# Squares of the residual: two instructions of 2048 columns behind the first pair of column tiles, in place of eight of 512 inside it

## The chip, the cores and the metric

The kernel runs on one core of one Trainium2 chip. The metric is device time in microseconds (us) of one execution, as a median over several. A core has TensorE (PE, matmuls), VectorE (DVE), ScalarE (ACT), GpSimd (POOL) and SyncE (SP, which issues most DMAs). Each takes its own instructions strictly in the order in which the program was laid down; an instruction that waits holds up all that stand behind it on its engine.

## The reference

One decoder layer on 256 positions of 2048 channels in float32. The part that matters here is its second half:

```python
h = h + rms_norm(m @ w_out[l], post_mix_gain[l], NORM_EPS)
u = rms_norm(h, pre_ff_gain[l], NORM_EPS)
f = jnp.square(jax.nn.relu(u @ w_ff1[l])) @ w_ff2[l]
h = h + rms_norm(f, post_ff_gain[l], NORM_EPS)
```

`rms_norm(x, gain)` is x times gain divided by the root of the mean of the squares of x over the 2048 channels. For the second line the mean of h squared is wanted, one number for each of the 256 positions. `w_ff1` is 2048 x 8192, `w_ff2` 8192 x 2048.

## The kernel before, in words

Every float32 weight is used as a sum of two parts: ACT rounds it to a first part (`wh`, L141) and DVE takes the remainder (`wl`, L147), and TensorE multiplies with both. Weights come as chunks of 128 x 2048 (1 MB) from DRAM into one of three raw buffers; there are three buffers for `wh` and three for `wl`. In the first feed-forward product a chunk is a column tile: 128 of the 8192 output columns, over all 2048 channels. For each, PE does sixteen matmuls of 512 columns with `wh` (L272, the "high" half) and sixteen of 256 with `wl` (L276, the "low" half). Two column tiles make a pair (`ws_pair`, L267 to L281) that fills one PSUM tile `ps`; ACT and DVE then read it (L284, L285), and DVE multiplies it with `r2b`, the reciprocal root of the mean square (L877).

The norm's factor isn't applied to h ahead of the product, but to the product: so PE can start on the raw h. The first pair of column tiles, here called c0 and c1, is done in `stream` (L326 to L351), which for each of 16 blocks of 128 channels transposes h on PE (L333), scales it with the gain on ACT (L245) and DVE (L246), and multiplies (L260, L263). At fixed points in it `second_hook` (L688) puts other work: the last pieces of h itself on DVE (L681, `mix_out`), the split of the third column tile c2, and the squares: after every fourth block two ACT instructions over 512 columns each (`square`, L684), one for each half of the positions, whose sums land in `hss`. After the stream DVE adds up `hss` (L718), ACT takes the root (L315), DVE the reciprocal (L316) and a diagonal matrix from it (L722, `dg`); two small matmuls (L723) spread it over all partitions, and ACT copies it to `r2b` (L724).

The PSUM tile that L723 writes belongs to a pool that is closed right after (L729); its banks are then given to a new pool (L730), and from then on pairs take their PSUM tile from the old pool and the new one in turn. So a pair in the new pool can't start before L724 has read the factor; the pair behind it uses the old pool, and can start when the stream's own PSUM tile has been read (L284, L285).

Counting column tiles from c0: the stream does c0 and c1, the first pair behind it c2 and c3, the next ones c4 and c5, then c6 and c7, and so on.

Instructions marked with `pin` keep their order among themselves as written. All others are placed by a scheduler that simulates the program with estimated times when it is built, and lets an engine take a later piece of work first if by the estimate an earlier one would wait. The buffers for `wh` and `wl` are handed out in the order that it finds.

## Time and profile before

| what | us |
|---|---|
| median of 3 runs (1537.08 to 1538.44) | 1537.52 |
| the profiled execution, as timed | 1537.91 |
| its span, first to last instruction | 1536.1 |
| PE busy in it | 1519.5 |
| DVE busy | 1274.4 |
| ACT busy | 786.6 |

The busy time of an engine sums the durations of its instructions. A matmul's end is modelled, so neighbours overlap: a stretch in which PE is wholly busy can still differ in speed, which the granted clock and the distance between starts show. In a timeline each row is a run of like instructions: its start, how long it lasted, and in brackets how long the engine had idled before it and what ended that.

### The profile page before, as it was taken

The page shows a single profiled execution, that of the slowest core. Times are in us where ns is not written, and L with a number is a line of the kernel's source. Part 1 is how long each engine was busy: PE and PEld are TensorE (multiplying, and loading weights), DVE is VectorE, ACT ScalarE, POOL GpSimd, SP SyncE. Part 2 cuts the span into 40 slices and gives each one's busy share as a digit, 9 for nine tenths or more (in the row PEclk, how much of TensorE's full clock was granted, in tenths as well). Part 3 has the DMA queues.
Part 4 walks back from the last instruction along what each step waited for, and adds up shares of the span by engine and source line. Part 5 has one row for each costly group of instructions (what it writes and reads, how often), then busy time and mean ns, then how long its engine had stood idle before and what let it go on. Part 6 is the DMA issues. An engine that isn't in the chain of part 4 may idle for free.

```text
span 1536.1 us, 19418 instructions
## 1 busy us (share of the span) xinstructions
PE 1519.5 (99%) x7714; PEld 1293.0 (84%) x7714; DVE 1274.4 (83%) x1611; ACT 786.6 (51%) x857; POOL 42.2 (3%) x73
## 2 busy tenths in 40 slices
PE   9999999999999999999999999999999999999997
PEld 8888888888888888888887888888888888788885
DVE  8999999999999997956546888867887778867888
ACT  7544454655554545733435545644455445644454
POOL 0000000000000000000000000000011000110010
PEclk9999999999999999999999999999999999999999
DMA  8655555454544555575454654685478755795673
GB/s 325 221 192 187 185 186 184 167 189 165 192 165 169 205 202 192 186 280 184 180 194 168 247 179 184 215 271 189 166 223 269 225 185 185 238 294 192 233 228 129
DMA packets 51771, 313.66 MB, mean 204 GB/s; under 512 B 5728, under 2 KB 5856, under 8 KB 17248
## 3 DMA queue, kind: packets, MB, share of 16 engines
q1 hardware_dynamic: 44640, 290.40, 52.4%
q0 software_dynamic: 7040, 22.02, 6.1%
q8 instruction: 60, 0.98, 0.3%
q14 instruction: 31, 0.25, 0.0%
HBM read 295.62 MB, written 4.19 MB: 195 GB/s over the span
## 4 chain that ended last, share of the span: by engine, by line
PE 92%; DVE 3%; ACT 2%; issue 1%; DMA 0%; SPq 0%; DVEq 0%; ACTq 0%
PE ps L272 30%; PE ps L276 15%; PE ps L294 9%; PE ps L295 9%; PE ps L293 9%; PE ps L812 4%; PE ps L813 4%; PE ps L811 3%; DVE wl L147 2%; ACT wh L141 2%; PE ps L782 2%; PE ps L781 2%; PE ps L784 2%; PE po L548 1%; PE ps L260 1%
## 5 line engine op out<-in xcount | busy, mean ns | idle before, releaser
L141 ACT CAST wh<-raw 128x2048 fp32r<-128x2048 f32 (+1 forms) x256 | 456.6, 1790 | 487.5 <-PE ps L295 162.6
L147 DVE TENSOR_TENSOR wl<-raw,wh 128x2048 fp32r<-128x2048 f32 (+1 forms) x256 | 546.7, 2140 | 187.5 <-ACT wh L141 182.7
L272 PE MATMUL ps<-act,wh 128*128 128x512 f32 x1984 | 479.4, 392 | 0.0
L272 PEld LDWEIGHTS ps<-act,wh 128*128 128x128 f32 x1984 | 364.7, 188 | 70.1
L276 PEld LDWEIGHTS ps<-act,wl 128*128 128x128 f32 x1984 | 256.5, 191 | 10.0
L276 PE MATMUL ps<-act,wl 128*128 128x256 f32 x1984 | 263.8, 284 | 0.0
L294 PE MATMUL ps<-wl,act 128*128 128x512 f32 x624 | 243.8, 391 | 0.0
L293 PE MATMUL ps<-wh,act 128*128 128x512 f32 x624 | 243.7, 390 | 0.0
L295 PE MATMUL ps<-wh,act 128*128 128x512 f32 x624 | 243.6, 390 | 0.0
L462 DVE SCALAR_TENSOR_TENSOR y_all<-c,vec,y_all 128x256 f32<-128x256 f32 x480 | 210.1, 479 | 0.0
L294 PEld LDWEIGHTS ps<-wl,act 128*128 128x128 f32 x624 | 117.2, 188 | 24.1
L293 PEld LDWEIGHTS ps<-wh,act 128*128 128x128 f32 x624 | 117.2, 188 | 24.1
L295 PEld LDWEIGHTS ps<-wh,act 128*128 128x128 f32 x624 | 117.2, 188 | 24.0
L157 ACT CAST wh<-raw 128x1024 fp32r<-128x1024 f32 x64 | 65.3, 1051 | 91.2 <-PE ps L813 23.3
L812 PE MATMUL ps<-wl,g 128*128 128x512 f32 x256 | 101.4, 396 | 2.5 <-DVE wl L147 1.5
L813 PE MATMUL ps<-wh,g 128*128 128x512 f32 x256 | 99.8, 390 | 0.0
L811 PE MATMUL ps<-wh,g 128*128 128x512 f32 x256 | 99.7, 389 | 0.0
L782 PE MATMUL ps<-wl,gs 128*128 128x512 f32 x224 | 87.5, 391 | 0.6 <-DVE wl L158 0.5
L781 PE MATMUL ps<-wh,gs 128*128 128x512 f32 x224 | 87.2, 389 | 0.0
L784 PE MATMUL ps<-wh,gs 128*128 128x512 f32 x224 | 87.2, 389 | 0.0
L158 DVE TENSOR_TENSOR wl<-raw,wh 128x1024 fp32r<-128x1024 f32 x64 | 76.4, 1220 | 3.1 <-ACT wh L157 1.9
L157 ACT CAST wh<-sum 128x1024 fp32r<-128x1024 f32 x48 | 49.1, 1052 | 38.6 <-PE ps L272 14.3
(206 smaller groups left out, 1260.6 us busy)
## 6 DMA issues: line engine op xcount, KB each, us to landing
raw<-in_w_f_dram SPq DMA_DIRECT2D x124, 1024.0 KB, 5.0
raw<-in_w_q_dram SPq DMA_DIRECT2D x16, 1024.0 KB, 4.8
raw<-in_w_k_dram SPq DMA_DIRECT2D x16, 1024.0 KB, 4.8
raw<-in_w_v_dram SPq DMA_DIRECT2D x16, 1024.0 KB, 4.8
raw<-in_w_ga_dram SPq DMA_DIRECT2D x16, 1024.0 KB, 4.9
raw<-in_w_gc_dram SPq DMA_DIRECT2D x16, 1024.0 KB, 4.8
raw<-in_w_co_dram SPq DMA_DIRECT2D x16, 1024.0 KB, 4.8
raw<-in_w_o_dram SPq DMA_DIRECT2D x16, 1024.0 KB, 4.8
```

Of the source, the lines that this page charges most:

```text
L141: i = nc.scalar.copy(wh[:, a:b], raw[:, a:b])
L147: i = (eng or nc.vector).tensor_sub(wl[:, a:b], raw[:, a:b], wh[:, a:b].bitcast(F32))
L272: a = nc.tensor.matmul(ps[:, j], wh[:, k * P:(k + 1) * P], acts.both(k), start=(k == 0), stop=False)
L276: a = nc.tensor.matmul(ps[:, j, S:], wl[:, k * P:(k + 1) * P], acts.hi(k), start=False, stop=(k == KT - 1))
L293: nc.tensor.matmul(ps, acts.hi(k, a, b), wh[:, sl], start=(k == 0), stop=False)
L294: nc.tensor.matmul(ps, acts.hi(k, a, b), wl[:, sl], start=False, stop=False)
L295: nc.tensor.matmul(ps, acts.lo(k, a, b), wh[:, sl], start=False, stop=(k == KT - 1))
L462: i = nc.vector.scalar_tensor_tensor(y, c[:, j:j + S], vcol(ct, V_DW + j), y, op0=ALU.mult, op1=ALU.add)
L782: pin(nc.tensor.matmul(ps, g[:, 0, a], wl[:, sl], start=False, stop=False))
L811: pin(nc.tensor.matmul(ps, ga.hi(k, a, b), wh[:, sl], start=first, stop=False))
L812: pin(nc.tensor.matmul(ps, ga.hi(k, a, b), wl[:, sl], start=False, stop=False))
L813: pin(nc.tensor.matmul(ps, ga.lo(k, a, b), wh[:, sl], start=False, stop=last))
```

## The change

The function `square`, its call in `second_hook`, the tile `hss` and its sum on DVE go. In their place two ACT instructions of 2048 columns stand behind the stream, pinned there; each leaves the whole sum of one half of the positions in `r2`. As target for the squares themselves, which nobody reads, they use `y_sb`, whose last reader is `mix_out` in the stream and whose next writer is the second feed-forward product.

```diff
-    hss = fin.tile([P, NT, NB], F32, name="hss")
...
-    def square(t, n):
-        sq = fin2.tile([P, 2, S], F32, name="z").rearrange("p a t -> p (a t)")
-        pin(nc.scalar.activation(sq, h_sb[:, t, n * 512:(n + 1) * 512], AF.Square, accum_out=hss[:, t, n:n + 1]))
-
     def second_hook(j, i):
...
-        if i == 3:
-            for t in range(NT):
-                square(t, j)
...
     dg = fin.tile([P, NT, P], F32, name="dg")
-    nc.vector.tensor_reduce(r2, hss, axis=AX.X, op=ALU.add)
+    for t in range(NT):
+        pin(nc.scalar.activation(y_sb[:, t], h_sb[:, t], AF.Square, accum_out=r2[:, t:t + 1]))
     rsqrt(r2, r2, epsn, 1.0 / D)
```

The orders of SP and POOL stay as they were; those of ACT, DVE and PE change behind the stream, where the scheduler places the rest anew. In the changed kernel lines behind the change have numbers lower by 7 (L724 is L717 there, L723 is L716).

On ACT, from the last squares of the stream in the kernel before; `wh_6914` is c3 (four pieces), `wh_6938` c4, `wh_7022` c5, `wh_7060` c6, `ps_6735` the PSUM tile of the stream and `ps_6989` that of c2 and c3:

```order
L686 ACTIVATE z_6903,hss_6195<-h_sb_6188 128x512
L315 ACTIVATE r2_6944<-r2_6944,epsn_93 128x2
L141 CAST wh_6914<-raw_6909 128x512 x4
L141 CAST wh_6938<-raw_6924 128x2048
L284 COPY z_6977<-ps_6735 128x512
L724 COPY r2b_6945<-aux_6950 128x256
L141 CAST wh_7022<-raw_6926 128x2048
L141 CAST wh_7060<-raw_6928 128x2048
L284 COPY z_7066<-ps_6989 128x512
```

The same place in the changed kernel; `wh_6897` is c3, `wh_6921` c4, `wh_7006` c5, `wh_7044` c6, `wh_7095` c7, `ps_6734` the PSUM tile of the stream, `ps_6973` that of c2 and c3:

```order
L141 CAST wh_6897<-raw_6892 128x512 x4
L141 CAST wh_6921<-raw_6907 128x2048
L711 ACTIVATE y_sb_6184,r2_6927<-h_sb_6188 128x2048 x2
L284 COPY z_6961<-ps_6734 128x512
L141 CAST wh_7006<-raw_6909 128x2048
L141 CAST wh_7044<-raw_6911 128x2048
L315 ACTIVATE r2_6927<-r2_6927,epsn_93 128x2
L284 COPY z_7050<-ps_6973 128x512
L141 CAST wh_7095<-raw_6925 128x2048
L717 COPY r2b_6928<-aux_6934 128x256
```

The two squares stand behind the cast of c4; the stream's PSUM tile is read only after them, then c5 and c6 are cast, and the copy of the factor follows after the cast of c7, where before it stood ahead of the cast of c5.

On PE, the end of the pair c2 and c3 and what follows, in the kernel before (`wl_6915` is c3's low half, `wh_6938` and `wl_6939` are c4, `wh_7022` is c5):

```order
L723 MATMUL aux_6950<-dg_6946,ones_102 128x128 x2
...
L276 MATMUL ps_6989<-act_6890,wl_6915 128x256 x2
L272 MATMUL ps_7078<-act_6745,wh_6938 128x512 x2
...
L276 MATMUL ps_7078<-act_6890,wl_6939 128x256 x2
L272 MATMUL ps_7078<-act_6745,wh_7022 128x512 x2
```

The same in the changed kernel (`wl_6898` is c3's low half, `wh_7044` and `wl_7045` are c6, `wh_7095` is c7, `wh_6921` c4):

```order
L276 MATMUL ps_6973<-act_6877,wl_6898 128x256 x2
L272 MATMUL ps_7151<-act_6744,wh_7044 128x512 x2
...
L276 MATMUL ps_7151<-act_6744,wl_7045 128x256 x2
...
L716 MATMUL aux_6934<-dg_6929,ones_102 128x128 x2
L272 MATMUL ps_7151<-act_6744,wh_7095 128x512 x2
...
L272 MATMUL ps_7062<-act_6744,wh_6921 128x512 x2
```

Behind c3 PE no longer takes c4 and c5, which now stand in the PSUM pool that waits for the copied factor, but c6 (both halves), then the two small matmuls of the factor, then the high half of c7, then c4 and c5, and the low half of c7 after them. From c8 on the order is as before.

## Rows read from the trace of the kernel before

**Rows 1.** The page, part 1: busy time, share of the span and instructions of each engine.
```profile
PE 1519.5 (99%) x7714; PEld 1293.0 (84%) x7714; DVE 1274.4 (83%) x1611; ACT 786.6 (51%) x857; POOL 42.2 (3%) x73
```

**Rows 2.** Waits of PE, whole span: us in total, times, longest.
```profile
PE aux L333 <- DVE h_sb L681: 1.5, 2, 1.3
PE ps L812 <- DVE wl L147: 1.5, 2, 1.1
```

**Rows 3.** Stretches: length, busy PE, PEld, DVE, ACT, POOL; clock, DMA share, GB/s.
```profile
827.00:830.50 3.50, 1.54 (x7) 0.75 (x7) 2.95 (x7) 2.41 (x7) 0.00 (x0) 1.00 0.49 206
830.60:834.00 3.40, 3.40 (x13) 2.86 (x12) 2.66 (x6) 2.19 (x7) 0.00 (x0) 0.50 0.00 0
834.00:850.00 16.00, 16.00 (x97) 14.04 (x96) 11.23 (x24) 12.76 (x32) 1.06 (x2) 1.00 0.54 190
```

**Rows 4.** Timeline of ACT, 845 to 862 us: start, us, instruction, [idle before, releaser].
```profile
845.34 0.62 ACT L686 ACTIVATE z<-h_sb 128x512 f32<-128x512 f32 x1
845.86 0.19 ACT L686 ACTIVATION_READ_ACCUMULATOR z<-h_sb 128x1 f32 x1
845.95 0.62 ACT L686 ACTIVATE z<-h_sb 128x512 f32<-128x512 f32 x1
...
847.63 3.99 ACT L141 CAST wh<-raw 128x512 fp32r<-128x512 f32 x5 [0.44 <-PE ps L260]
851.52 0.57 ACT L284 COPY z<-ps 128x512 f32<-128x512 f32 x1
852.00 0.37 ACT L724 COPY r2b<-aux 128x256 f32<-128x256 f32 x1
853.79 1.92 ACT L141 CAST wh<-raw 128x2048 fp32r<-128x2048 f32 x1 [1.43 <-DMA raw<-in_w_f_dram]
856.70 1.91 ACT L141 CAST wh<-raw 128x2048 fp32r<-128x2048 f32 x1 [0.99 <-DMA raw<-in_w_f_dram]
...
861.33 1.91 ACT L141 CAST wh<-raw 128x2048 fp32r<-128x2048 f32 x1 [2.24 <-PE ps L272]
```

**Rows 5.** ACT, 830 to 850 us, by form: busy, mean ns, idle before.
```profile
L686 ACT ACTIVATE z<-h_sb 128x512 f32<-128x512 f32 x8 | 4.9, 622 | 0.0
L245 ACT ACTIVATE act<-aux,gff 128x256 fp32r<-128x256 f32 x14 | 6.6, 472 | 3.8 <-PE aux L333 3.8
L141 ACT CAST wh<-raw 128x2048 fp32r<-128x2048 f32 x1 | 1.9, 1902 | 0.0
```

**Rows 6.** Line 414, squares of 1024 columns: ns least, median, most.
```profile
L414 ACT ACTIVATE xsq<-lead x3: 1045/1045/1063, 19.4 to 23.8; 128x1024 f32<-128x1024 f32 x3
```

**Rows 7.** Timeline of PE, 849.6 to 864 us.
```profile
849.55 1.35 PE L276 MATMUL ps<-act,wl 128*128 128x256 f32 x10
850.75 0.60 PE L723 MATMUL aux<-dg,ones 128*128 128x128 f32 x4
...
851.91 3.82 PE L272 MATMUL ps<-act,wh 128*128 128x512 f32 x16
855.57 2.08 PE L276 MATMUL ps<-act,wl 128*128 128x256 f32 x16
857.48 3.82 PE L272 MATMUL ps<-act,wh 128*128 128x512 f32 x16
861.13 2.08 PE L276 MATMUL ps<-act,wl 128*128 128x256 f32 x16
```

**Rows 8.** Timeline of DVE, 845 to 862 us.
```profile
847.42 0.48 DVE L722 TENSOR_SCALAR dg<-ident,r 128x128 f32<-128x128 f32 x2
...
851.65 2.29 DVE L147 TENSOR_TENSOR wl<-raw,wh 128x2048 fp32r<-128x2048 f32 x1 [0.87 <-ACT wh L141]
853.86 0.68 DVE L285 TENSOR_TENSOR z<-z,ps 128x512 f32<-128x512 f32 x1
```

**Rows 9.** The chain that ended last, 829 to 836 us: start, us, what.
```profile
832.32 0.43 PE ps L272
...
834.88 0.23 PE ps L272
```

## Prediction

> **What bounds the kernel now.** I read the page's busy times first, then the waits of PE, then the stretch of the change by windows, and then the timelines of ACT, PE and DVE at its place. PE is busy for 1519.5 of 1536.1 us [rows 1], and over the whole span its longest wait is 1.3 us [rows 2]: the kernel is bound by PE, and a change elsewhere costs or brings something only if PE comes to wait, or stops waiting. PE's largest hole in this half is ahead of the stream, where it works 1.54 us of 3.5 [rows 3]; there it waits for h. The squares begin behind that hole. [...]

> **What is removed.** Eight squares of 622 ns [rows 5], whose starts lie 0.61 us apart (845.34 and 845.95 [rows 4]; a read of the sum, 0.19 us, overlaps both neighbours): 8 x 0.61 = 4.9 us of ACT, and one short sum on DVE. Their cover is PE's own work, which doesn't stop, so I cost their removal at nothing. [...]

> **What is added, on ACT.** Two squares of 2048 columns. No row shows that size. 512 columns take 622 ns [rows 5] and 1024 take 1045 [rows 6], so another 512 cost 0.42, and 2048 take 1.05 + 2 x 0.42 = 1.89 us; with the read of the sum the starts lie 1.88 apart (0.01 less than the duration, as at 512), for two 3.8 us. Bounds: not under the cast of 2048 columns, whose successor starts 1.80 after it (849.72 to 851.52, below), so 3.6; not over eight squares of 512, 4.9. I take 3.8, since two rows of the same function give it. Their target `y_sb` makes no wait: its last reader stands in the stream.

> **Where they stand.** The five casts from 847.63 on are c3 in four pieces and c4 [rows 4]; c4 takes 1.90 [rows 5] and they end at 847.63 + 3.99 = 851.62, so c4 starts at 849.72. The first of them waits for PE (0.44 <- L260), not for the squares ahead of it, so I leave it where it is. From here ACT goes strictly down its new list: the squares start at 851.52, where before the read of the stream's PSUM tile stood, and end at 855.28; that read takes 0.48 (851.52 to 852.00 [rows 4]), to 855.76; the cast of c5 goes to 857.56, and the cast of c6 runs for 1.91 us, to 859.47. Both raw chunks were there by 853.79 and 856.70, since before each cast waited for its DMA until then [rows 4]; so neither DMA decides any longer, for c6 with 0.86 us to spare. SP's and POOL's queues keep their order, and what releases the raw buffers up to c4 hasn't moved.

> **Who waits.** Behind c3 PE now takes c6 and not c4. Its order was made so that c4 and c5, whose PSUM tile needs the copied factor, come later. Before, c4 started at 857.48. The small matmuls of the factor stood ahead of that: the low half they cut took 851.91 - 849.55 = 2.36, against 857.48 - 855.57 = 1.91 for one without them [rows 7], so 0.45. Without them PE is ready for c6 at 857.03. The cast of c6 ends at 859.47; DVE started 0.03 after such a cast (851.65 after 851.62 [rows 4, 8]), so PE starts at 859.50. **The new wait is 859.50 - 857.03 = 2.5 us**; with the bounds of the squares 2.3 to 3.6. Below nothing it can't go: PE's work is the same, and nothing that it waited for before comes earlier. Queued behind it on PE is everything to the end.

> **What comes next, with its margin.** DVE reads the PSUM tile at 855.9 for 0.68, then does the remainders of c5 (from 857.7) and c6, 2.29 each with starts 2.21 apart (851.65 to 853.86 [rows 8]): c6's is ready at 862.2. PE needs it behind the high half of c6, 859.50 + 3.65 = 863.15 (855.57 less 851.91 is 3.66 [rows 7]). Then DVE does the reciprocal, the read of c2 and c3 (0.68) and the diagonal (0.48 [rows 8]), to 863.6; PE wants it at 863.15 + 1.91 = 865.06: 1.4 to spare. The cast of c7 gets its buffer when c6's high half is read, 0.20 behind the start of the low half (861.33 against 861.13 [rows 4, 7]), so 863.35 to 865.26, and PE comes to it at 865.06 + 0.45 = 865.5: 0.2 to spare. The copy of the factor follows at some 865.8, and c4 starts at 869. So there is one wait and not three, if these margins hold. The small matmuls cost 0.45 at their new place as before. Later nothing gives the time back: the casts that set PE's pace there are released by PE itself, and of waits that a later PE could swallow there are 1.5 us [rows 2], on DVE's remainders, which move along.

> **The clock.** PE fell to half clock behind the hole at 827 to 830.5 and stayed there for the 3.40 us of the next row [rows 3]; a matmul of 512 columns then took 0.43 in the chain, against 0.23 at full clock [rows 9], so 3.4 us at half clock lose about 1.7. The new wait is an idle piece of 2.5 us, the hole before had 3.50 - 1.54 = 2.0 us idle, though in pieces; but ahead of the new wait PE has been full since 834 [rows 3, 7]. The trace shows no single wait of this length, so I put the fall somewhat below even and keep it as a rival. [...]

> **The sum.** 0 for what goes, 2.5 for the wait: 1537.91 + 2.5 = 1540.4 against the profiled execution's own time, whose span of 1536.1 leaves 1.8 around it that I leave alone. The median of the runs is 0.4 under the profiled one, so for a median: **1540.0 us**, 0.16% slower. About 0.2%, 3.1 us, is what a measurement of this kernel can tell from no change; so the likeliest case is slower by less than that.

> **The rivals.**
> - **The wait pulls the clock down** (the other side). [...] It decides from 0.6 us of loss on, where the sum passes 3.1. For it: the one hole of like idle time in the trace did so. Against it: the above. Runs may differ in it.
> - **A second wait**: c7's cast with its 0.2 us, or the DMA of c6 with its 0.86. A cast that comes one place later costs its 1.9, so 1541 to 1543. For it: thin margins. Against it: each is released by PE or was there earlier before.
> - **No wait**: ACT comes to c6 by 857.0, because in the new order something I place behind the squares runs ahead of them. 1537.5. Against it: ACT's list is fixed, and it would have to be 2.5 us shorter.
> - **The stream gets faster.** If the squares held PE in the stream unseen, under matmul ends that are modelled, at most their 4.9 us come back; with the wait that is 1535.1, without it 1532.6. Two instructions also cost ACT less than eight: 4.9 - 3.8 = 1.1 us. [...] Against the rival: 16.00 of 16 busy at full clock, and ACT's 3.8 us of waits for PE.

> **How the numbers follow.** The wait alone 0.48, with the clock 0.35, a second wait 0.06, no wait 0.06, a faster stream 0.05. Slower by over 0.2%: the clock, the second wait, and 0.04 of the first case for squares that come near their upper bound: 0.45. Faster by over 0.2%: 0.04 of the last case. Within: 0.51. The likeliest case alone spans 1539.8 to 1541.1 (2.3 to 3.6). The range for 8 in 10 takes in the clock and most of a second wait, and leaves out no wait and the faster stream: 1538.7 to 1543.0.

> **What would show it.** In the profile of the changed kernel: PE idle before the first L272 behind c3, some 2.5 us, ended by an ACT cast; on ACT, two squares of about 1.9 us from 851.5 on and the read of the stream's tile at 855.3; no idle time of PE at the small matmuls or at c7; PE still full from 834 to 850, at the same start of c3's high half, 851.5. Right behind the wait the clock shows 1.00, or 0.50 for the rival. I am wrong if PE doesn't wait there, if the wait is named after a DMA, or if the stream ends earlier by more than half a microsecond.

## The result, and the profile after

| | median us | runs | least to most us |
|---|---|---|---|
| before, on the same chip | 1537.44 | 4 | 1537.08 to 1538.44 |
| changed | 1547.01 | 4 | 1546.59 to 1547.86 |

The changed kernel takes 1.0062 times the time before (95% interval 1.005 to 1.0074): 9.6 us more, where 2.5 were forecast, and outside the range given. The profiled execution took 1546.59 us; its span is 1544.8 against 1536.1, so 8.7 us are to be found between the two traces.

The page of the changed kernel, part 1, as in [rows 1]:

```profile
PE 1527.8 (99%) x7714; PEld 1293.2 (84%) x7714; DVE 1274.0 (82%) x1610; ACT 786.5 (51%) x845; POOL 42.1 (3%) x73
```

PE is busy for 8.3 us more with the same 7714 instructions, although a wait alone adds no busy time. The longest waits of PE in the changed kernel, as in [rows 2]:

```profile
PE ps L272 <- ACT wh L141: 2.4, 1, 2.4
PE aux L333 <- DVE h_sb L680: 1.5, 2, 1.3
PE aux L378 <- POOL ident masks.py:199: 1.4, 1, 1.4
PE ps L805 <- DVE wl L147: 1.1, 1, 1.1
```

There is one new wait, of the predicted size (the one at L378, at the start of the program, is as long before). So the loss has two parts: one at the place of the change, which the waits show, and one elsewhere, which they don't.

**The part at the place.** PE in the changed kernel from 848 us, as in [rows 7] (the tile in 853.84 is c3's low half, that in 858.32 c6's high half):

```profile
848.28 2.07 PE L276 MATMUL ps<-act,wl 128*128 128x256 f32 x16
850.19 3.82 PE L272 MATMUL ps<-act,wh 128*128 128x512 f32 x16
853.84 2.07 PE L276 MATMUL ps<-act,wl 128*128 128x256 f32 x16
858.32 5.53 PE L272 MATMUL ps<-act,wh 128*128 128x512 f32 x16 [2.40 <-ACT wh L141]
863.69 2.07 PE L276 MATMUL ps<-act,wl 128*128 128x256 f32 x16
865.60 0.60 PE L716 MATMUL aux<-dg,ones 128*128 128x128 f32 x4
```

ACT at the same place, as in [rows 4]:

```profile
850.30 1.92 ACT L711 ACTIVATE y_sb<-h_sb 128x2048 f32<-128x2048 f32 x1
852.12 0.18 ACT L711 ACTIVATION_READ_ACCUMULATOR y_sb<-h_sb 128x1 f32 x1
852.21 1.90 ACT L711 ACTIVATE y_sb<-h_sb 128x2048 f32<-128x2048 f32 x1
854.01 0.18 ACT L711 ACTIVATION_READ_ACCUMULATOR y_sb<-h_sb 128x1 f32 x1
854.10 0.56 ACT L284 COPY z<-ps 128x512 f32<-128x512 f32 x1
854.57 3.70 ACT L141 CAST wh<-raw 128x2048 fp32r<-128x2048 f32 x2
```

The squares start 1.91 us apart and hold ACT for 3.80 (850.30 to 854.10). The two casts of the last row are c5 and c6, and end at 858.27; PE starts at 858.32. Its high half then takes 5.53 us instead of 3.82. The stretches say why (length, then busy PE, PEld, DVE, ACT, POOL; granted clock, DMA share, GB/s), and stand against [rows 3]:

```profile
827.00:830.50 3.50, 1.54 (x7) 0.79 (x7) 2.95 (x7) 2.41 (x7) 0.00 (x0) 1.00 0.45 190
830.60:834.00 3.40, 3.40 (x20) 2.67 (x19) 3.34 (x8) 1.76 (x4) 0.00 (x0) 1.00 0.00 0
858.90:862.30 3.40, 3.40 (x10) 2.63 (x9) 3.15 (x5) 0.03 (x1) 0.00 (x0) 0.50 0.70 234
```

Behind the wait PE ran at half clock (granted 0.50) for some 3.4 us. In this execution the clock did not fall (granted 1.00) behind the hole of 827 to 830.5, which has the same 1.54 us of work as before: from 830.6 to 834 it did 20 matmuls, where it did 13 [rows 3]. So the stream ended 1.27 us earlier (848.28 against 849.55 [rows 7]). By c8, whose high half starts at 882.72 against 879.75, the changed kernel is 3.0 us behind: the wait's 2.4 and the clock's 1.7 less 1.3 at the hole, and 0.2 between.

**The part elsewhere: 8.7 - 3.0 = 5.7 us.** PE's groups by form from 880 us on (count, then busy us, mean ns of one, idle before) show where. The second feed-forward product before:

```profile
L811 PE MATMUL ps<-wh,g 128*128 128x512 f32 x256 | 99.7, 389 | 0.0
L781 PE MATMUL ps<-wh,gs 128*128 128x512 f32 x224 | 87.2, 389 | 0.0
```

and in the changed kernel, where these lines are L804 and L774:

```profile
L804 PE MATMUL ps<-wh,g 128*128 128x512 f32 x256 | 101.1, 395 | 0.0
L774 PE MATMUL ps<-wh,gs 128*128 128x512 f32 x224 | 88.5, 395 | 0.0
```

Its 1440 matmuls are recorded 5 to 6 ns longer, by the mean of each line. They overlap (389 ns long before, 0.227 us from start to start), so their pace is read from the distance of starts. Before, at the end of the span (29 distances from the first row to the last, 6.57 us, 0.227 each):

```profile
1519.78 0.39 PE L811 MATMUL ps<-wh,g 128*128 128x512 f32 x1
...
1526.35 0.39 PE L813 MATMUL ps<-wh,g 128*128 128x512 f32 x1
```

and changed (31 distances, 7.23 us, 0.233 each):

```profile
1527.74 0.40 PE L805 MATMUL ps<-wl,g 128*128 128x512 f32 x1
...
1534.97 0.39 PE L806 MATMUL ps<-wh,g 128*128 128x512 f32 x1
```

Over the whole product the mean of such distances (without the gaps, 0.26 us and more) is 0.2271 before and 0.2333 after, and all its distances together are 334.3 and 339.9 us: 5.6 more. The clock is not it: from 1105 to 1175 us it is 1.00 in both, with less DMA traffic in the changed kernel than before (before first, then changed):

```profile
1105.00:1175.00 70.00, 69.72 (x303) 56.21 (x302) 62.16 (x50) 39.44 (x36) 5.97 (x7) 1.00 0.72 234
```
```profile
1105.00:1175.00 70.00, 70.00 (x298) 55.23 (x298) 59.54 (x49) 39.93 (x37) 5.12 (x6) 1.00 0.65 210
```

298 matmuls in the time of 303, with PE full. These are the same instructions, in an order the change does not touch, 250 us behind it. What differs is where their operands lie. `hss`, removed, held 32 bytes of each partition in the pool `fin`; every tile allocated behind it (`r2b`, `dg`, `z`, `gs`, `g` and more) moved down by 32, while the weight tiles `wh` and `wl` and the tiles `act`, allocated ahead of it, stayed. In the built programs `wh` and `wl` start at bytes that leave 224 modulo 256 in both kernels; `g` and `gs` leave 224 before and 192 after. The second product is the one that multiplies `g` and `gs` with `wh` and `wl`: `g` or `gs` is the operand of the weight load ahead of a matmul (the stationary one; at L811 before a load is 128x128 and takes 188 ns), `wh` or `wl` the one of the matmul itself (the moving one; 128x512, 389 ns). The parts of a tile that single matmuls read begin at whole multiples of 512 bytes in it, so a tile's first byte gives the remainder for all of them. The tiles `act` leave 224 in both, and the products that read them keep their time (L272 from 880 us on: 391 ns before, 390 after).

### The profile page after: what moved, and what is told of

Its sections match the earlier page's. It is cut to its first block, busy times and chain, and to the rows that moved or that the text cites. A ratio compares the mean times of both kernels' runs of the same rounds, so it can differ in the third digit from the quotient of the medians.

```text
span 1544.8 us, 19403 instructions
## 1 busy us (share of the span) xinstructions
PE 1527.8 (99%) x7714; PEld 1293.2 (84%) x7714; DVE 1274.0 (82%) x1610; ACT 786.5 (51%) x845; POOL 42.1 (3%) x73
## 4 chain that ended last, share of the span: by engine, by line
PE 96%; DVE 2%; ACT 1%; issue 1%; DMA 0%; SPq 0%; DVEq 0%; ACTq 0%
PE ps L272 29%; PE ps L276 15%; PE ps L294 9%; PE ps L293 9%; PE ps L295 9%; PE ps L805 4%; PE ps L806 4%; PE ps L804 4%; PE ps L774 3%; PE ps L775 3%; PE ps L777 3%; PE po L548 1%; PE ps L260 1%; DVE wl L158 0%; PE s L520 0%
## 5 line engine op out<-in xcount | busy, mean ns | idle before, releaser
L272 PE MATMUL ps<-act,wh 128*128 128x512 f32 x1984 | 480.2, 393 | 2.4 <-ACT wh L141 2.4
L272 PEld LDWEIGHTS ps<-act,wh 128*128 128x128 f32 x1984 | 365.5, 189 | 73.3 <-ACT wh L141 2.6
L804 PE MATMUL ps<-wh,g 128*128 128x512 f32 x256 | 101.1, 395 | 0.0
L774 PE MATMUL ps<-wh,gs 128*128 128x512 f32 x224 | 88.5, 395 | 0.0
```

What stands on the lines that cost most here:

```text
L272: a = nc.tensor.matmul(ps[:, j], wh[:, k * P:(k + 1) * P], acts.both(k), start=(k == 0), stop=False)
L804: pin(nc.tensor.matmul(ps, ga.hi(k, a, b), wh[:, sl], start=first, stop=False))
```

## Experiments

My theory after the result: the move of the squares costs the local part alone, and the 32 bytes cost the rest, by the place of `g` and `gs` against the weights (the place theory). The rivals: the slower product follows from the moved squares, by other arrival times of weights (the order theory); or a tile's own place counts, not the place of one against the other. An added tile named `room` is never read or written; kernels that differ from their base by it alone keep their base's order of instructions. Each ratio is against the kernel before on the same chip: 1537.91 us for e1, e2, e3 and e6, 1537.32 for e4, e5, e7 and e8, 1537.6 for e9 and e10.

**e1_room_after.** The changed kernel with 32 bytes left where `hss` was.

```
     ypre = fin.tile([P, NT], F32, name="ypre")
+    fin.tile([P, NT, NB], F32, name="room")
```

> The changed kernel with an unused tile of 32 bytes per partition where hss stood, so that every tile behind it in SBUF lies where it lay before the change; the order of instructions is that of the changed kernel. Place theory (the matmuls of the second feed-forward product go slower because their stationary operand g moved by 32 bytes): starts of 512-column matmuls there 0.227 us apart again in place of 0.234, and the time falls from 1547.0 to about 1541 (the wait of 2.4 us, the half clock behind it, and what the stream gains or loses by its own half clock, are left). Order theory (the new order or the new handing out of weight buffers slows them): 0.234 and 1547 as they are.

Measured: 1540.84 us (1540.41 to 1542.71) against 1537.91 before, ratio 1.0022 (1.0013 to 1.0031). The distance in the second product is 0.2271 again, and the wait stays:

```profile
858.12 5.55 PE L272 MATMUL ps<-act,wh 128*128 128x512 f32 x16 [2.35 <-ACT wh L141]
```

So the moved squares cost 2.9 us, and the slower product does not come from them.

**e2_room_before.** The kernel before, squares in their place, with 32 bytes behind `hss`, which moves `g` and `gs` up by 32.

```
     hss = fin.tile([P, NT, NB], F32, name="hss")
+    fin.tile([P, NT, NB], F32, name="room")
```

> The kernel before with an unused tile of 32 bytes per partition behind hss: same order of instructions as the kernel before, but g and all else behind it moved by 32 bytes, while the weight buffers stay. Place theory: matmuls of the second feed-forward product 0.234 apart, no new wait of PE behind the stream, time about 1543 to 1544 (the 5.7 us that the changed kernel lost behind c8). Order theory: 0.227 and 1537.5.

Measured: 1543.41 us (1542.07 to 1544.33), ratio 1.0035 (1.0022 to 1.0047), without any new wait. One of its groups:

```profile
L812 PE MATMUL ps<-wh,g 128*128 128x512 f32 x256 | 101.3, 396 | 0.0
```

An unused tile alone makes the kernel 5.5 us slower, with the distances of the changed kernel (0.2333).

**e3_room_first.** The kernel before, with the 32 bytes ahead of all tiles, so that weights, `act`, `g` and `gs` all move up together.

```
+    const.tile([P, NT, NB], F32, name="room")
     epsn = const.tile([P, 1], F32, name="epsn")
```

> The kernel before with an unused tile of 32 bytes per partition ahead of all others: weight buffers, act, g, all move by 32 bytes together. Place theory in the form that the two operands of a matmul must lie in the same half of 64 bytes: nothing changes, 0.227 and 1537.5. Place theory in the form that a stationary operand at a multiple of 64 is slow: 0.234 in the second feed-forward product, in the stages whose stationary operand is act or wh as well, and a time of 1543 to 1555. Order theory: 1537.5.

Measured: 1538.06 us (1536.44 to 1539.95), ratio 1.0001 (0.9992 to 1.0009), distance 0.227. The place by itself does not count.

**e6_room_both.** The edits of e2 and e3 together: the weights move up by 32, `g` and `gs` by 64.

```
+    const.tile([P, NT, NB], F32, name="room")
...
+    fin.tile([P, NT, NB], F32, name="room")
```

> The kernel before with both unused tiles, one ahead of all others and one behind hss: weight buffers and act moved by 32 bytes, g by 64, so that g lies in its old half of 64 bytes and the weights in the other. Place theory, both operands in the same half: 0.234 in the second feed-forward product and about 1543 to 1544. Place theory, stationary operand at a multiple of 64: the second feed-forward product keeps 0.227 and the stages with act as stationary operand go to 0.234. Order theory: 1537.5.

Measured: 1542.6 us (1542.3 to 1543.8), ratio 1.0032 (1.0019 to 1.0044), distance 0.2333: slow as in e2, where the same 32 bytes lie between the two. The place of one operand against the other decides.

**e8_room_g_alone.** The kernel before, with the 32 bytes between `gs` and `g`, so that `g` moves and `gs` stays.

```
     gsp = ctx.enter_context(tc.tile_pool(name="gsp", bufs=2 * FAST))
+    ctx.enter_context(tc.tile_pool(name="roomp", bufs=1)).tile([P, NT, NB], F32, name="room")
     gpool = ctx.enter_context(tc.tile_pool(name="gpool", bufs=KT // 2 - 2 * FAST))
```

> The kernel before with an unused tile of 32 bytes just ahead of the pool of g: g moves by 32 bytes (with tmp and ev behind it), while gs, sc, sum, z and the weight buffers stay. Place theory: in the second feed-forward product the matmuls with g (L813 to L815 here) go to 0.234, those with gs (L783 to L786) stay at 0.227; of 768 x 0.007 = 5.4 us a part is swallowed by waits, time 1539.5 to 1542. Rival (it is what ACT and DVE read and write there, sc, sum or z, whose place matters): both stay at 0.227 and 1537.5 to 1538.

Measured: 1541.6 us (1540.18 to 1542.27), ratio 1.0028 (1.0017 to 1.0039). Within one execution the matmuls with `g` are slow and those with `gs` are not:

```profile
L812 PE MATMUL ps<-wh,g 128*128 128x512 f32 x256 | 101.2, 395 | 0.0
L785 PE MATMUL ps<-wh,gs 128*128 128x512 f32 x224 | 87.4, 390 | 0.0
```

768 matmuls by 6.1 ns are 4.7 us; 4.3 were measured. So it is the place of these operands: `tmp` and `ev`, which moved along with `g`, are read by no matmul.

**e7_room_64, e9_room_128, e10_room_256.** The kernel before, with 64, 128 and 256 bytes behind `hss`: how far until it is fast again?

```
+    fin.tile([P, 2 * NT, NB], F32, name="room")
```

> The kernel before with an unused tile of 64 bytes per partition behind hss: g and all behind it move by 64 bytes. Place theory, both operands in the same half of 64 bytes: as before, 0.227 us between starts and 1537.5 to 1538. Rival (any move of g, or more room taken, slows the matmuls; or the period is longer than 64 bytes): 0.234 and about 1543.

Measured with 64: 1543.47 us (1542.7 to 1544.24), ratio 1.004 (1.0027 to 1.0054), distance 0.2334. The expectation, a period of 64, missed. The next two have `4 * NT` and `8 * NT` in the same line.

> The kernel before with an unused tile of 128 bytes per partition behind hss. So far 0 bytes of shift between weights and g was fast (also with both moved by 32), 32 and 64 were slow. Period of 128 bytes: 0.227 us between starts in the second feed-forward product and 1537 to 1538. Longer period, or any shift but none: 0.233 and about 1543.

Measured with 128: 1543.11 us (1541.47 to 1543.46), ratio 1.0033 (1.0022 to 1.0044), distance 0.2329.

> The kernel before with an unused tile of 256 bytes per partition behind hss. Period of 128 or 256 bytes: 0.227 us and 1537 to 1538; with e9_room_128 slow, a period of 256. Longer period, or any shift but none: 0.233 and about 1543.

Measured with 256: 1537.13 us (1536.31 to 1538.13), ratio 0.9997 (0.9987 to 1.0006), distance 0.2272, and its group has the time of before:

```profile
L812 PE MATMUL ps<-wh,g 128*128 128x512 f32 x256 | 99.7, 390 | 0.0
```

All together, by the place of `g` less that of the weights, against the kernel before:

| bytes | kernels | distance of starts, us |
|---|---|---|
| 0 | before, e1, e3 | 0.2271, 0.2271, 0.227 |
| -32 | changed | 0.2333 |
| +32 | e2, e6, e8 (`g` alone) | 0.2333, 0.2333, 0.2332 |
| +64 | e7 | 0.2334 |
| +128 | e9 | 0.2329 |
| +256 | e10 | 0.2272 |

Fast where both operands start at the same byte modulo 256, slow at each other place that was tried (all of them multiples of 32).

**e4_squares_twice.** e1 with each square done twice, to double the suspected hold-up of ACT.

```
     for t in range(NT):
-        pin(nc.scalar.activation(y_sb[:, t], h_sb[:, t], AF.Square, accum_out=r2[:, t:t + 1]))
+        for again in range(2):
+            pin(nc.scalar.activation(y_sb[:, t], h_sb[:, t], AF.Square, accum_out=r2[:, t:t + 1]))
```

> The changed kernel with the 32 bytes put back (as e1_room_after) and each of the two squares done twice, four instructions of 2048 columns. Of them three now stand ahead of the cast of c6 on ACT, one behind it. Theory of the wait (PE stands behind c3 until the cast of c6, which the squares push back by 1.89 us each): PE waits 2.4 + 1.9 = 4.3 us there, time 1.9 above e1_room_after, about 1542.7. Rival (the wait is set by the DMA of c6's raw chunk or by PE's own order): 2.4 us and 1540.8 as in e1_room_after.

Measured: 1543.81 us (1543.44 to 1544.09) against 1537.32 before, ratio 1.0042 (1.0029 to 1.0056). Three of the four squares come ahead of c6's cast, and PE's wait grew by the 1.9 us of the third:

```profile
861.08 6.68 PE L272 MATMUL ps<-act,wh 128*128 128x512 f32 x16 [4.26 <-ACT wh L141]
```

The time is 1.1 us above what was expected, and 1.7 when e1 and e4 are each taken against the kernel before on their own chip (2.9 and 6.5 us more). The stretches name the clock: it fell behind the hole too, as in [rows 3], and stayed down behind the longer wait for twice as long as behind the wait of 2.4 us (6.70 us at a granted 0.50, against 3.40 in the changed kernel):

```profile
829.60:832.90 3.30, 3.00 (x11) 2.52 (x11) 3.29 (x7) 1.61 (x4) 0.00 (x0) 0.50 0.00 0
...
860.30:867.00 6.70, 5.92 (x14) 4.68 (x15) 3.44 (x5) 3.41 (x5) 0.00 (x0) 0.50 0.61 229
```

Not all of that stretch is loss, since PE still waited in its first 0.78 us.

**e5_old_banks.** e1 with the order of PSUM pools shifted by one, so that c4 and c5 take the pool that needs no copied factor, as before, and follow c3 again; the squares stay behind the casts of c3 and c4.

```
         for j in range(KT // 2):
+            pi[0] += q == 0 and j == 2
             ps = ws_pair(u2) if q or j else lead_ps
```

> The changed kernel with the 32 bytes put back and the turn of the two PSUM pools shifted by one from the second pair on: c4 and c5 get the stream's PSUM tile in the old pool, and c6 and c7 are the first that need the copied factor. PE then takes c4 behind c3. Theory of the wait: c4 is cast long before, its PSUM tile is read by 856.6, PE wants it at 857.0, so no wait there (at most 0.5 us later, ahead of c8's high half), and with the squares out of the stream at no gain the time is that of the kernel before, 1537.5 to 1538. Rival (the squares behind the stream cost by themselves, as ACT work that comes late): 1539 or more. Rival (squares in the stream held PE unseen): 1533 to 1536.

Measured: 1536.53 us (1535.89 to 1538.22) against 1537.32 before, ratio 0.9997 (0.9988 to 1.0005). c4, cast ahead of the squares, is there when PE comes (its high half starts at 855.72), and PE has no idle time from 834 to 900:

```profile
853.80 2.08 PE L276 MATMUL ps<-act,wl 128*128 128x256 f32 x16
855.72 3.82 PE L272 MATMUL ps<-act,wh 128*128 128x512 f32 x16
```
```profile
834.00:900.00 66.00, 66.00 (x389) 58.47 (x388) 48.74 (x61) 36.99 (x42) 1.06 (x2) 1.00 0.61 220
```

So the 2.9 us of e1 need the order in which c6 follows c3: with c4 there, the same two squares at the same place cost nothing that can be measured, and taking the squares out of the stream brings nothing that can be measured. This is the fastest median of all kernels run, but not apart from the kernel before.

## Why the prediction was wrong, step by step

**The step that failed: what is removed.** I costed the removal of eight squares and `hss` "at nothing", with PE's own work as the cover. That counted instructions. `hss` was also 32 bytes of memory ahead of other tiles, and its removal cost some 5.5 us: 5.6 by the starts in the two traces, and e2, which makes such a shift alone, takes 5.5 more. Nothing covers it, because it lies on PE itself. The edit of one line that I gave no row and no range was worth twice the rest.

**The new wait** was right: 2.40 us against 2.5, named after ACT's cast of c6, and 2.35 in e1. The three terms in it held: squares 1.91 apart (1.88), the read of the stream's tile behind them, both casts released by ACT's own order and not by a DMA.

**The margins** held. The waits name no second one at the diagonal, the small matmuls or c7.

**The faster stream** was rightly given little. The stream did end 1.27 us earlier, which I had named as a sign against me; but that is the clock in the hole, since e4 has the moved squares and the fall (granted 0.50 from 829.6 to 832.9), and e10 has the squares in the stream and no fall there (1.00 from 827 to 834).

**The clock** was put somewhat below even and came about: right behind the wait 0.50 was granted, for 3.40 us in the changed kernel (858.9 to 862.3) and over the stretch of 3.30 us in e1 (859.6 to 862.9). The likeliest case took 0 for it where 1.7 us is right behind that wait. In the profiled run of e1 that was partly given back at the hole (granted 1.00 from 827 to 834, where the kernel before had 0.76); over all runs e1 is 2.9 us slower, with an interval of 2.0 to 4.8 that holds both my 2.5 and the 4.2 of the rival with the clock (2.5 for the wait and 1.7). Two executions that both kept the full clock at the hole (1.00 from 827 to 834) side with the rival. The high half of c8 in e10, whose squares stand in the stream, and in e1:

```profile
878.43 3.82 PE L272 MATMUL ps<-act,wh 128*128 128x512 f32 x16
```
```profile
882.59 3.82 PE L272 MATMUL ps<-act,wh 128*128 128x512 f32 x16
```

e1 is 4.2 us later there, which is the wait's 2.35, the clock's 1.7 and 0.1 between. So for the part at the place the sum with the clock was the right one, and it was the term of the clock, taken as 0, that my likeliest case had too small. In the changed kernel the high half of c6 took 5.53 for 3.82, which is 1.71.

**"Later nothing gives the time back"** is nearly right. The slower pace alone would be 1402 distances by 6.2 ns, 8.7 us; 3.2 of these went into gaps between tiles that PE had before anyhow (what it lost there fell from 8.1 to 4.9 us), as the wait for DVE at line 812 [rows 2] fell from 1.5 to 1.1. Here the slower PE swallowed waits on the others, but only those it had.

**No rival gave this**, because each asked when an instruction can start and, the clock's apart, none how fast it runs once it has started. With the place of tiles kept (e1), 2.9 us more were measured where 2.5 were forecast. That this is so near is in part luck, since my 2.5 held nothing for the clock; why the medians lie 2.9 apart and not 4.2 is open, though the fall at the hole, which comes in some executions only, is of the size that is missing.

**One reading** was wrong without consequence: PE's longest wait before is not the 1.3 us of [rows 2] but one of 1.4 at L378, at the start of the program.

## What to carry to other kernels

A tile that is added or removed moves all tiles behind it: compare the operands' addresses of the two programs, and leave an unused tile of the same size in its place when the edit itself is to be measured. Where the engine that sets the time is busy for longer with the same instructions, compare the distance of their starts by group, far from the edit as well; the waits of PE did not show it here. In matmuls like these (512 columns, fp32r), let the stationary and the moving operand start at the same byte modulo 256, where the starts lay 0.227 us apart and not 0.233, and check which tile the bound engine takes next before work is put ahead of that tile's cast.
